# A planner of instruction order is given a margin behind the landing of loads and a limit on side products

## The chip, the cores and the metric

The kernel runs on one core of a Trainium2 chip. The metric is the device time of one execution in microseconds (us), given as the median of several runs; a profile of one further execution is read beside it.

## What is computed

Two layers of a hybrid decoder trunk, for a prompt of 256 tokens and for 8 sample tokens (one step each), all in float32. Each layer is

```python
h = rms_norm(x, norm_w)
z = einsum('btd,dc->btc', h, w_in)                 # 2048 -> 7296 columns, split among the branches
y_a = rwkv_time_mix(z_a, ...)                      # 12 heads x 64: token shift, delta-rule matrix state, group norm
y_b = attention_branch(z_b, ...)                   # 12 heads x 64: dilated windows (prompt), cache of past rows (sample)
y_c = pool_branch(z_c, ...)                        # causal multi-scale mean pooling
mix = concatenate([y_a, y_b, y_c])                 # each branch multiplied by SiLU of its own gate columns
y = x + einsum('btc,cd->btd', mix, w_out)          # 2048 -> 2048
```

and the new states (matrix state, shifted row, pooling rows, new keys and values) are outputs too.

## The kernel before

Work is held with channels on the 128 partitions and the 264 tokens (256 + 8) in the free dimension. The two big projections are the **stream** (`stream`, line 301): weights come in pieces of 512 KB (`raw`, four blocks of 128 rows by 256 columns, three buffers), ScalarE rounds a piece to float32r (`hi`), VectorE makes the rest (`lo <- raw - hi`), and TensorE adds hi x xh, hi x xl and lo x xh into a PSUM tile of tag `acc` (three buffers, two of them in use for a pair of column tiles). A stream matmul is 128x128 by 128x264. In the output projection the moving operands are the mix tiles `mh`/`ml` (branch A), `mb` (branch B) and `mc` (branch C), and `stream` takes the quarters in the order 2, 1, 3, 0, so that the later half of `mb` is read first.

All other TensorE work is **side products**, into PSUM tiles of tag `a` (five buffers): transposes, the low-rank products, the delta-rule chunks, the attention scores and values. The parts of a layer follow each other in the program like this:
- `up_load` loads the raw up matrices (`rwkv_w_up`, `rwkv_a_up`), which are cast to `up`; the scale of the rows (`x_done`, `row_scale`, tiles `ss`, `rtok`, `dg`, `rstd`) is made in the same stretch, and every projected tile `z` is multiplied by `rstd`.
- `a_k`, `a_kdone`, `a_r`, `a_solve` build the chunk matrices. They go through DRAM (`g_dram`) and come back as `xm`, which a loop of 15 steps on VectorE inverts in blocks of 16 (tile `tm`); the results go through DRAM again and come back as `ra`, `rat`, `rb`, `rbt` (in the tile `iv`), `x16` and `x32`.
- `invert` (line 525) makes the inverses of 64 x 64 from these by four products, each of 12 x 4 small matmuls: `x16` with `rat`, `y16` with `right`, `x32` with `rbt`, `y32` with `rb`. Then `a_chain` runs the chunks.
- `b_prompt` is the attention of the prompt and `b_sample` that of the sample tokens. `b_sample` takes six pairs of `kc` (cache, by GpSimd's queue) and `qb` (queries spread over the partitions, by SyncE's queue) and then three groups of two `vc`; all these tiles have the tag `c4` with three buffers.
- `a_mix`, `b_mix`, `c_gate` write the mix tiles; then comes the output projection.

The order of the instructions on each engine is not that of the program. After the program is built, the class `Plan` (line 1336) takes all instructions, their dependences, the buffer rings and a cost for each, and simulates the engines (`once`, line 1554): at each point of plan time every free engine takes the ready instruction with the longest tail of work behind it. `apply` then fixes each engine's order by this plan. On the chip an engine runs its queue strictly in that order and waits where an operand is late.

TensorE has two ready lists in the plan, stream and side. A side product is begun when a run of them is on, when one has been ready for `wait` = 1500 ns, or when `batch` = 400 ns of them are ready; else a stream matmul is taken, and if there is none, a side product after all. A `bundle` is a row of side matmuls that is kept together (`self.after`, `forced`). A load is taken to land at a modelled time (`fin`), and its consumers become ready `slack` later: 0 for what the stream itself needs (`feeds`: the operands of stream matmuls' own predecessors such as the casts), `care` = 1200 ns on TensorE and `margin` = 200 ns elsewhere. The plan is made twice: after the first pass no load that isn't a weight piece may be issued earlier than 12 us before its first consumer (`ahead`).

Of the kernel before, what the change touches and what calls it, by code (L numbers as in the profile page):

```python
# [3 lines left out]

# [1331 lines left out]
class Plan:  # L1336
# [200 lines left out]
                tail[q] = max(tail[q], t)  # L1537
        return tail

    def run(self, factor=1, hop=300, margin=200, batch=0, wait=0, switch=0, quiet=0, lead=1, dyn=(), ahead=0, care=350):  # L1540

        self.hold = [0.0] * self.n
        args = factor, hop, margin, batch, wait, switch, quiet, lead, dyn, care
        if ahead:
            self.once(*args)
            for k, i in enumerate(self.ins):
                if self.dma[k] and not self.feeds(k):
                    self.hold[k] = max(0.0, min([self.start[q] for q in self.after_load[k]], default=0.0) - ahead)
        return self.once(*args)
# [1 line left out]
    def feeds(self, k):  # L1551
        return self.tag[self.first_out[k]].startswith("raw") if self.first_out[k] in self.tag else False

    def once(self, factor, hop, margin, batch, wait, switch, quiet, lead, dyn, care):
        n, eng, preds, dma, dur, stream = self.n, self.eng, self.preds, self.dma, self.dur, self.stream
        spare = {t: d for t, r in self.ring.items() for m, d in dyn if t.split("_" + self.pool[r[0]])[0] == m}
        tail = self.tails(factor, hop, spare)
# [2 lines left out]
        feeds = {q for k in range(n) if stream[k] for q in preds[k]}  # L1560
        slack = [0 if stream[k] or k in feeds else care if eng[k] == "PE" else margin for k in range(n)]
# [32 lines left out]
        hw = bus_free = now = 0.0  # L1594
        start, fin, order = [0.0] * n, [0.0] * n, {e: [] for e in free}
        taken = {"DVE": 0.0, "POOL": 0.0}
        release = []
        last_use = defaultdict(float)
        done, since, side_on, last_stream, forced = 0, None, False, False, None
        claims = {k: [t for t in ts if t in left] for k, ts in self.claim.items()}  # L1600
# [15 lines left out]
        def take(h):  # L1616
            while h:
                p, k = heapq.heappop(h)
                w = blocked(k)
                if w is None:  # L1620
                    return k
                parked[w].append(k)
            return None

        def unpark(key):
            for k in parked.pop(key, ()):
                heapq.heappush(ready[queue(k)], (prio[k], k))

        while done < n:
            while pending and pending[0][0] <= now + 1e-9:  # L1630
                _, k = heapq.heappop(pending)
                heapq.heappush(ready[queue(k)], (prio[k], k))
            while release and release[0][0] <= now + 1e-9:
                _, t = heapq.heappop(release)
                free_slots[self.tag[t]] += 1
                open_tiles[self.pool[t]] -= 1
                unpark(self.tag[t])
                unpark("pool " + self.pool[t])
            moved = False
            for e in free:  # L1640
                if free[e] > now + 1e-9 or (e == "SP" and hw > now + 700):
                    continue
                if e == "PE" and forced is not None:
                    k = forced
                elif e == "PE":
                    h = ready["SIDE"]
                    if h and since is None:
                        since = now
                    k = None
                    if h:  # L1650
                        go = side_on or h[0][0] < -2e9 or now - since >= wait or sum(dur[x[1]] for x in h) >= batch
                        if go:
                            k = take(h)
                            if k is not None:
                                side_on = True
                                since = None
                    if k is None:
                        k = take(ready["PE"])
                        if k is None and h:
                            k = take(h)  # L1660
                        if k is not None and stream[k]:
                            side_on = False
                            since = since if h else None
                else:
                    k = take(ready[e])
                if k is None:
                    continue
                for t in claims.get(k) or touches[k]:
                    if t not in live:
                        live.add(t)  # L1670
                        tag = self.tag[t]
                        while next_tile[tag] < len(self.ring[tag]) and self.ring[tag][next_tile[tag]] in live:
                            next_tile[tag] += 1
                        free_slots[tag] -= 1
                        unpark(tag)
                start[k] = now
                if dma[k]:
                    if e == "SP":
                        hw = max(hw, now) + 470
                        free[e] = now + 60  # L1680
                        begin = max(hw + 650, bus_free)
                    else:
                        free[e] = now + 520
                        begin = max(now + 1690, bus_free)
                    bus_free = begin + bust[k]
                    fin[k] = bus_free + 908
                else:
                    extra = 0
                    if e == "PE" and stream[k] != last_stream:
                        extra = switch if stream[k] else 0 if k in claims else switch / 2  # L1690
                    elif self.port[k]:
                        extra = max(0.0, taken["POOL" if e == "DVE" else "DVE"] - now)
                    free[e] = fin[k] = now + dur[k] + extra
                    if self.port[k]:
                        taken[e] = fin[k]
                if e == "PE":
                    last_stream = stream[k]
                    forced = self.after.get(k)
                order[e].append(k)
                done += 1  # L1700
                moved = True
                out = list(succ[k])
                if stream[k]:
                    nstream += 1
                    out += held.pop(nstream, ())
                for q in out:
                    r = fin[k] if dma[k] else fin[k] + (100 if eng[q] == "SP" else HOP[e, eng[q]])
                    if e != eng[q] or dma[k]:
                        r += slack[q]
                    est[q] = max(est[q], r)  # L1710
                    count[q] -= 1
                    if not count[q] and q != forced:
                        heapq.heappush(pending, (est[q], q))
                for t in touches[k]:
                    left[t] -= 1
                    last_use[t] = max(last_use[t], fin[k] + (0 if dma[k] else 150 if e == "PE" else 100))
                    if not left[t]:
                        heapq.heappush(release, (last_use[t], t))
            if moved:
                continue  # L1720
            c = [x for x in free.values() if x > now + 1e-9]
            if pending:
                c.append(pending[0][0])
            if release:
                c.append(release[0][0])
            if hw > now + 700:
                c.append(hw - 700)
            c = [x for x in c if x > now + 1e-9]
            if not c:
                raise RuntimeError(f"no order found: {done} of {n} {dict((a, len(b)) for a, b in parked.items())}")  # L1730
            now = min(c)
# [68 lines left out]
def build(nc, shapes, depth=DEPTH):  # L1800
    ins = {n: nc.dram_tensor(f"in_{n}", s, F32, kind="ExternalInput").ap() for n, s in shapes.items()}
    outs = {n: nc.dram_tensor(f"out_{n}", s, F32, kind="ExternalOutput").ap() for n, s in _OUTS}
    with tile.TileContext(nc, schedule_with_timeline_sim=True) as tc, ExitStack() as ctx:
        trunk = Trunk(ctx, tc, ins, outs, depth)
        trunk.run()
        plan = Plan(tc, trunk.bundles)
        plan.run(ahead=12000, care=1200, batch=400, wait=1500, switch=105, margin=200, hop=180, factor=0.9, lead=25, quiet=60, dyn=[("a", 2)])
        plan.apply()


# [10 lines left out]
```

## Time and profile before

| | us |
|---|---|
| median of 3 runs | 1086.47 |
| lowest and highest run | 1085.95, 1093.89 |
| the profiled execution's own time | 1087.3 |
| its span, first to last instruction | 1085.5 |
| TensorE busy in it (share) | 1045.3 (96%) |
| VectorE, ScalarE busy | 856.8 (79%), 546.3 (50%) |
| mean granted TensorE clock | 0.992 |

The span is the time between the first and the last instruction; the execution's own time also holds what lies around it. Layer 0 lasts to about 552 us of the span, layer 1 from there to the end.

### The profile page before, as it was taken

To read this page: it belongs to the slowest core of one execution; us is meant where nothing else is said; L and a number is where in the kernel's file an instruction comes from. 1 tells how busy PE (TensorE), PEld (TensorE's weight loads), DVE (VectorE), ACT (ScalarE), POOL (GpSimd) and SP (SyncE) were. 2 spreads that over 40 slices of the span, in tenths; PEclk is the share of its full clock that TensorE was granted. 3 is DMA by queue.
4 is the path that set the end of the run, shared out by engine and by line. 5 is a ranking of instruction groups with operands and counts; after the bars stand their busy time and mean duration, and the time that the engine had idled before them with its cause. 6 is when DMAs were issued, how large, how long until landed. Compare 5 with 4: busy or idle time off the path is not lost.

```text
span 1085.5 us, 24558 instructions
## 1 busy us (share of the span) xinstructions
PE 1045.3 (96%) x9802; PEld 997.2 (92%) x9802; DVE 856.8 (79%) x1684; ACT 546.3 (50%) x934; POOL 136.3 (13%) x262
## 2 busy tenths in 40 slices
PE   9999999889998999999999999989999999989998
PEld 8899898889897987999999998989898998979998
DVE  7769977989997898766666799689997999886443
ACT  7546434354655474444545464334537465734332
POOL 0003210100012101000110042112000231010000
PEclk9999999999999999999999999999999999999999
DMA  7654489797467865577775545797984488655774
GB/s 273 203 156 144 148 250 247 212 237 233 135 190 244 267 186 179 178 231 224 228 238 160 174 133 174 229 263 214 254 239 137 149 255 297 204 177 173 232 226 149
DMA packets 154683, 223.64 MB, mean 206 GB/s; under 512 B 75984, under 2 KB 109152, under 8 KB 154552
## 3 DMA queue, kind: packets, MB, share of 16 engines
q1 hardware_dynamic: 146456, 195.94, 60.5%
q0 software_dynamic: 8112, 26.12, 7.2%
q8 instruction: 77, 1.26, 0.5%
q14 instruction: 38, 0.31, 0.1%
HBM read 198.55 MB, written 24.03 MB: 205 GB/s over the span
## 4 chain that ended last, share of the span: by engine, by line
PE 53%; DVE 23%; DMA 12%; issue 5%; ACT 5%; SPq 1%; DVEq 0%; ACTq 0%; POOLq 0%
PE acc L323 46%; DVE lo L140 7%; PE a L115 6%; DMA raw<-in_w_in 3%; DMA qb<-q_dram 2%; ACT hi L137 2%; PE a L118 2%; DVE z L140 2%; SPq L155 1%; DVE tm L140 1%; DMA svec<-sk_dram 1%; DVE s L140 1%; DMA rwkv_a_up<-in_rwkv_a_up 1%; DMA res<-resid 1%; DMA q_dram<-brows 1%
## 5 line engine op out<-in xcount | busy, mean ns | idle before, releaser
L323 PE MATMUL acc<-xh,hi 128*128 128x264 f32 x1824 | 473.2, 289 | 6.6 <-DVE z L140 3.3
L323 PE MATMUL acc<-xl,hi 128*128 128x264 f32 x1824 | 473.2, 290 | 0.0
L137 ACT ACTIVATE hi<-raw 128x1024 fp32r<-128x1024 f32 (+1 forms) x296 | 309.8, 1046 | 323.1 <-PE acc L323 228.2
L140 DVE TENSOR_TENSOR lo<-raw,hi 128x1024 fp32r<-128x1024 f32 (+1 forms) x296 | 356.9, 1206 | 137.2 <-ACT hi L137 136.2
L323 PEld LDWEIGHTS acc<-xh,hi 128*128 128x128 f32 x1824 | 346.0, 190 | 12.8 <-ACT hi L137 4.4
L323 PEld LDWEIGHTS acc<-xl,hi 128*128 128x128 f32 x1824 | 346.2, 190 | 5.0 <-issue 3.7
L323 PE MATMUL acc<-xh,lo 128*128 128x264 f32 x1824 | 295.6, 289 | 2.3 <-DVE lo L140 2.1
L323 PEld LDWEIGHTS acc<-xh,lo 128*128 128x128 f32 x1824 | 249.9, 190 | 8.1 <-DVE lo L140 3.9
L323 PE MATMUL acc<-mb,hi 128*128 128x264 f32 x384 | 57.3, 284 | 0.3 <-DVE xs L140 0.2
L140 DVE TENSOR_TENSOR z<-acc,rstd 128x264 f32<-128x264 f32 (+1 forms) x112 | 51.7, 466 | 5.2 <-ACT rstd L137 2.1
L323 PEld LDWEIGHTS acc<-mb,hi 128*128 128x128 f32 x384 | 50.9, 188 | 0.8 <-DVE xs L140 0.8
L323 PE MATMUL acc<-mh,hi 128*128 128x264 f32 x192 | 49.5, 284 | 0.0
L323 PE MATMUL acc<-ml,hi 128*128 128x264 f32 x192 | 49.4, 285 | 0.0
L353 POOL COPY zcol<-z 128x9 f32<-128x9 f32 x50 | 20.2, 404 | 219.1 <-DVE z L140 209.6
L323 PEld LDWEIGHTS acc<-ml,hi 128*128 128x128 f32 x192 | 36.2, 188 | 0.0
L323 PEld LDWEIGHTS acc<-mh,hi 128*128 128x128 f32 x192 | 36.1, 188 | 0.0
L323 PE MATMUL acc<-mb,lo 128*128 128x264 f32 x192 | 33.8, 285 | 0.0
L323 PE MATMUL acc<-mh,lo 128*128 128x264 f32 x192 | 33.6, 283 | 0.0
L323 PE MATMUL acc<-mc,hi 128*128 128x264 f32 x256 | 33.5, 283 | 0.0
L323 PEld LDWEIGHTS acc<-mc,hi 128*128 128x128 f32 x256 | 32.0, 188 | 0.0
L140 DVE TENSOR_TENSOR xs<-acc,res 128x264 f32<-128x264 f32 x32 | 13.5, 433 | 22.1 <-DMA res<-resid 16.0
L323 PEld LDWEIGHTS acc<-mh,lo 128*128 128x128 f32 x192 | 27.6, 188 | 0.0
(357 smaller groups left out, 1309.1 us busy)
## 6 DMA issues: line engine op xcount, KB each, us to landing
raw<-in_w_in SPq DMA_DIRECT2D x224, 512.0 KB, 3.6
raw<-in_w_out SPq DMA_DIRECT2D x64, 512.0 KB, 3.6
g_dram<-gs SPq DMA_DIRECT2D x8, 768.0 KB, 6.9
gs<-g_dram SPq DMA_DIRECT2D x8, 768.0 KB
kc<-in_cache_k_w POOLq DMA_DIRECT2D x12, 512.0 KB, 5.6
qb<-q_dram SPq DMA_DIRECT2D x12, 512.0 KB, 4.5
vc<-in_cache_v_w POOLq DMA_DIRECT2D x12, 512.0 KB, 4.5
s<-in_state_wkv POOLq DMA_DIRECT2D x12, 256.0 KB, 4.3
```

The source lines that it names most:

```text
L115: self.note(self.nc.tensor.matmul(out, lhsT, rhs, start=start, stop=stop))
L118: self.note(self.nc.tensor.transpose(out, in_, self.c("ident")[base:base + k, base:base + k]))
L137: self.nc.scalar.activation(out, in_, func, **kw)
L140: self.nc.vector.tensor_tensor(out, a, b, op=op)
L155: self.nc.sync.dma_start(out, in_)
L323: self.nc.tensor.matmul(accs[t][:, :T], a[:, k4, cs], b[k], start=first, stop=q == order[3] and k4 == 3 and late == 1)
L353: self.nc.gpsimd.tensor_copy(self.zcol[:, :, a], z[:, NP - 1:T])
```

## The change

Two parameters are added to the planner, and the call sets `far=1500` and `dense=100`. With `far`, a consumer of a load becomes ready 1500 ns later in the plan than before, unless it is one that the stream needs directly (`feeds`) or stands on SyncE or GpSimd. With `dense`, the planner keeps the begin times of all side matmuls of the last 8000 ns of plan time (`recent`), and does not take a side product ahead of the stream while there are 100 or more; the path that takes one because no stream matmul is ready, and the later members of a bundle, are as before. No instruction is added or removed.

```diff
@@ run, once: two more parameters
-    def run(self, factor=1, hop=300, margin=200, batch=0, wait=0, switch=0, quiet=0, lead=1, dyn=(), ahead=0, care=350):
+    def run(self, factor=1, hop=300, margin=200, batch=0, wait=0, switch=0, quiet=0, lead=1, dyn=(), ahead=0, care=350, far=0, dense=10 ** 9):
...
-        release = []
+        release, recent = [], deque()
...
                     k = None
-                    if h:
+                    while recent and recent[0] < now - 8000:
+                        recent.popleft()
+                    if h and len(recent) < dense:
                         go = side_on or h[0][0] < -2e9 or now - since >= wait or sum(dur[x[1]] for x in h) >= batch
...
                 if e == "PE":
                     last_stream = stream[k]
+                    if not stream[k]:
+                        recent.append(now)
                     forced = self.after.get(k)
...
                     if e != eng[q] or dma[k]:
-                        r += slack[q]
+                        r += slack[q] + (far if dma[k] and q not in feeds and eng[q] != "SP" and eng[q] != "POOL" else 0)
...
-        plan.run(ahead=12000, care=1200, batch=400, wait=1500, switch=105, margin=200, hop=180, factor=0.9, lead=25, quiet=60, dyn=[("a", 2)])
+        plan.run(ahead=12000, care=1200, far=1500, dense=100, batch=400, wait=1500, switch=105, margin=200, hop=180, factor=0.9, lead=25, quiet=60, dyn=[("a", 2)])
```

## Rows read from the trace of the kernel before

**Rows 1.** The page, part 1: busy us (share of the span) of TensorE and VectorE

```profile
PE   1045.3 (96%) x9802; PEld 997.2 (92%) x9802; DVE 856.8 (79%) x1684; ACT 546.3 (50%) x934; POOL 136.3 (13%) x262
```

**Rows 2.** TensorE in windows: length, busy us (matmuls), granted clock, DMA share, GB/s

```profile
40.00:48.00 8.00, 6.37 (x39) 0.79 0.33 91
...
216.00:224.00 8.00, 7.80 (x224) 0.79 1.14 249
...
760.00:768.00 8.00, 5.82 (x205) 0.96 1.09 267
768.00:776.00 8.00, 8.00 (x138) 0.83 0.89 251
...
968.00:976.00 8.00, 5.64 (x48) 0.97 0.78 261
976.00:984.00 8.00, 8.00 (x57) 0.82 0.45 132
```

**Rows 3.** TensorE's timeline: start, length, instruction, [idle time before it <- releaser]

```profile
42.37 0.39 PE L323 MATMUL acc<-xh,hi 128*128 128x264 f32 x1 [1.63 <-DVE z L140]
...
216.20 1.31 PE L115 MATMUL a<-rat,x 32*32 32x16 f32 x96 [3.68 <-DMA rat<-rat_dram]
...
226.22 1.02 PE L115 MATMUL a<-iv,x 32*32 32x32 f32 x96
...
229.37 0.37 PE L115 MATMUL a<-iv,y 32*32 32x32 f32 x18
...
232.29 0.87 PE L115 MATMUL a<-iv,y 32*32 32x32 f32 x78 [2.55 <-issue]
...
428.93 0.64 PE L115 MATMUL a<-vc,ppad 128*32 128x256 f32 x8 [1.32 <-DMA vc<-in_cache_v_w]
...
569.00 0.39 PE L323 MATMUL acc<-xh,hi 128*128 128x264 f32 x1 [0.95 <-DVE z L140]
...
755.20 0.99 PE L115 MATMUL a<-rat,x 32*32 32x16 f32 x96
...
765.47 1.17 PE L115 MATMUL a<-iv,x 32*32 32x32 f32 x96 [2.18 <-DVE s L140]
...
963.46 0.64 PE L115 MATMUL a<-vc,ppad 128*32 128x256 f32 x8 [0.40 <-DMA vc<-in_cache_v_w]
...
974.20 0.64 PE L115 MATMUL a<-vc,ppad 128*32 128x256 f32 x8 [1.72 <-DMA vc<-in_cache_v_w]
```

**Rows 4.** Who waited for whom: us in total, times, longest us

```profile
ACT ra L137 <- DMA ra<-ra_dram: 7.8, 2, 4.7
...
DVE kc L140 <- DMA qb<-q_dram: 5.8, 6, 1.8
...
ACT up L137 <- DMA rwkv_w_up<-in_rwkv_w_up: 4.0, 2, 2.2
DVE tm L140 <- DMA xm<-g_dram: 4.0, 2, 2.1
```

**Rows 5.** Instructions with mb, 400 to 470 us: durations ns, first and last start

```profile
L323 PE MATMUL acc<-mb,hi x32: 281/284/288, 457.5 to 469.9; 128*128 128x264 f32 x32
...
L140 DVE TENSOR_TENSOR mb<-sgb,mb x6: 419/427/434, 422.3 to 439.4; 128x264 fp32r<-128x264 f32 x6
```

**Rows 6.** The same for 960 to 1010 us (layer 1)

```profile
L323 PE MATMUL acc<-mb,hi x48: 281/284/323, 988.1 to 1004.5; 128*128 128x264 f32 x48
...
L140 DVE TENSOR_TENSOR mb<-sgb,mb x6: 425/426/434, 967.0 to 984.9; 128x264 fp32r<-128x264 f32 x6
```

**Rows 7.** DMA issues: count, KB each, median us from issue to landing

```profile
x<-x_dram SPq DMA_DIRECT2D x2, 192.0 KB, 5.1
```

**Rows 8.** SyncE's timeline at 760 us: start, length, instruction

```profile
760.25 0.43 SPq L155 DMA_DIRECT2D x<-x_dram  x1
```

**Rows 9.** ScalarE's timeline at 764 us

```profile
764.76 1.06 ACT L137 ACTIVATE hi<-raw 128x1024 fp32r<-128x1024 f32 x1 [3.61 <-DMA raw<-in_w_in]
```

More of the change, by code (lines that the diff above doesn't have):

```diff
@@ L1 @@
 import heapq
-from collections import Counter, defaultdict
+from collections import Counter, defaultdict, deque
 from contextlib import ExitStack, contextmanager
@@ L1538, in tails @@
         return tail
-    def run(self, factor=1, hop=300, margin=200, batch=0, wait=0, switch=0, quiet=0, lead=1, dyn=(), ahead=0, care=350):
+    def run(self, factor=1, hop=300, margin=200, batch=0, wait=0, switch=0, quiet=0, lead=1, dyn=(), ahead=0, care=350, far=0, dense=10 ** 9):
         self.hold = [0.0] * self.n
-        args = factor, hop, margin, batch, wait, switch, quiet, lead, dyn, care
+        args = factor, hop, margin, batch, wait, switch, quiet, lead, dyn, care, far, dense
         if ahead:
@@ L1552, in feeds, with once @@
         return self.tag[self.first_out[k]].startswith("raw") if self.first_out[k] in self.tag else False
-    def once(self, factor, hop, margin, batch, wait, switch, quiet, lead, dyn, care):
+    def once(self, factor, hop, margin, batch, wait, switch, quiet, lead, dyn, care, far, dense):
         n, eng, preds, dma, dur, stream = self.n, self.eng, self.preds, self.dma, self.dur, self.stream
```

## The prediction

> **What bounds the kernel now.** Four kinds of view, in this order. First the busy shares of the page: TensorE is busy 1045.3 us of the 1085.5 us span and VectorE 856.8 us [rows 1]. TensorE's work does not change (the edit touches only the order), so what can be won is the 40.2 us in which TensorE is idle, plus what its clock costs, and the rest is fixed. Second, TensorE alone in windows of 8 us [rows 2]: the granted clock is 0.79 in the window at 40 us, 0.79 at 216, 0.96 and 0.83 at 760 and 768, and 0.97 and 0.82 at 968 and 976. [...] Each costs (1 - 0.79) x 8 = 1.7 us of full-speed time (0.04 + 0.17 and 0.03 + 0.18 of a window make the same). Third, TensorE's instructions in order of time with the idle time before them [rows 3]: before each of those falls stands a gap, 1.63, 3.68, 2.18 and 1.72 us long. A gap that goes or gets much shorter therefore gives back its own length and perhaps 1.7 us more. Fourth, who waits for loads [rows 4]: ScalarE waits 7.8 us for ra and 4.0 us for the first raw up matrix, over both layers, VectorE 5.8 us for qb and 4.0 us for xm. An engine runs its queue in order, so such a wait also holds the hi and lo casts behind it, and without casts TensorE's stream stops.
>
> The second thing to see is what the end of each layer hangs on. The last write of mb (the attention part of the mix) starts at 439.4 us in layer 0 and 984.9 us in layer 1 and takes 0.43 us; the first output matmul that reads mb starts at 457.5 and 988.1 us [rows 5, 6]. So the side chain ends 17.7 us early in layer 0 and only 2.8 us early in layer 1.
>
> **The margin behind landings (far).** It adds 1.5 us to the time at which the planner thinks a loaded tile can be used, for consumers on TensorE, ScalarE and VectorE that do not feed the stream directly. It adds no instruction and no wait. It moves these consumers back in their queue, behind other work that the plan has ready at that time; loads on SP and GpSimd are not given the margin themselves, though they follow the new order. The x32 load shows how late data really comes: 192 KB takes 5.1 us from issue to landing [rows 7]. A consumer that now stands at the head of a queue for longer than 1.5 us gets at most 1.5 us of that back, one that waits less gets all of it. By place, first layer 0:
> - up matrices: they stand in front of the chain that makes the row scale, and the first scaled z releases TensorE after 1.63 us at 42.37 [rows 3]. ScalarE waits 4.0 / 2 = 2.0 us there in a layer [rows 4], more than that, so the gap can go whole, and its clock fall with it: 1.63 + 1.7 = 3.3 us.
> - rat and ra: TensorE waits 3.68 us at 216.20 [rows 3], and ScalarE holds a hi cast behind ra. 1.5 us comes back; 2.2 us of gap stays, so I leave the clock fall in: 1.5 us (the other end is 3.68 + 1.7 = 5.4).
> - vc: 1.32 us at 428.93 [rows 3], all of it: 1.3 us.
> - xm: VectorE waits 2.0 us in each layer [rows 4], of which 1.5 us comes back to VectorE; it is busy 79% of the span [rows 1], so between nothing and 1.5 us reaches TensorE and I take the middle, 0.75 us.
>
> Layer 1: 0.95 us before the scaled z at 569.00, vc 0.40 us at 963.46 and 1.5 of the 1.72 us at 974.20 with its clock fall of 1.7 us [rows 2, 3], and 0.75 us for xm: 5.3 us. The gap of 2.18 us at 765.47 I count at nothing. It is put down to VectorE, but the product reads x32, whose load is issued at 760.25 and takes about 5.1 us [rows 7, 8], so it is a landing. Yet at the same time the next hi cast waits 3.61 us for its own raw tile and ends only at 765.8 [rows 9]: TensorE would have had nothing else to run. Its other end is 2.18 + 1.7 = 3.9 us.
>
> **The limit on side products (dense).** At most 100 side matmuls may begin in 8 us of plan time while a stream matmul is ready; the later members of a bundle are exempt, and so is TensorE with no stream work. The densest stretch is the block inverse, four products of 12 x 4 = 48 matmuls (a row counts 96: each fp32 matmul of the program is two in the trace). Two products fit under the limit, so the third may begin 8 us after the first at the earliest. On the chip it stands 226.22 - 216.20 = 10.0 us behind it in layer 0 and 765.47 - 755.20 = 10.3 in layer 1 [rows 3]; at that spacing the limit hardly binds. In the plan, which knows no late landing, the products may stand closer. So it costs the chain between nothing and 8 less two products of 1.31 us, 5.4 us; I take nothing, by the rows. What it may give: the fourth product stops for 2.55 us at 232.29, after 18 of its 96 equal matmuls, and the profile shows nothing that it waits for ("issue") [rows 3]. I read this as instructions that had not arrived, because the first 18 and the other 78 read the same two tiles. Spread out, they should not outrun their delivery: between 0 and 2.55 us, in layer 0 alone. As the limit binds so little I take half, 1.3 us. [...]
>
> **What both cost.** They make the side chain longer in the plan. In the sample attention six pairs of kc and qb go through three buffers one after the other: 6 x 1.5 = 9.0 us for each layer, of which 5.8 / 2 = 2.9 us is waited already [rows 4]; 6.1 is left. Three groups of vc make 3 x 1.5 = 4.5, less the 1.3 us waited in layer 0 and 2.1 in layer 1: 3.2 and 2.4. In layer 0 that is 9.3 us, with the limit's bound 14.7, against 17.7 us of early end [rows 5]: other stream work stands in front of the output matmuls, and the cost is nothing. In layer 1 it is 8.5 us against 2.8 [rows 6]: between 0 (the chain's own hops get shorter where queues wait less) and 5.7 us. No row decides between these ends, so I take the middle, 2.9 us.
>
> Sum: layer 0 gives 3.3 + 1.5 + 1.3 + 0.75 + 1.3 = 8.2 us, layer 1 gives 5.3 - 2.9 = 2.4: 10.6 us less. The profiled execution took 1087.3 us (1.8 us outside its span), 0.8 us above the median of 1086.47, so 1087.3 - 10.6 - 0.8 = 1076 us.
>
> **Rivals.** (1) The chain of layer 1 is not the bound, because work on it also loses its waits: both layers give their gains in full, 8.2 + 5.3 = 13.5, so 1073 us; with the rest of the gaps at 216.20, 232.29 and 765.47 and their clock falls (2.2 + 1.7 + 1.3 + 3.9 = 9.1) 1064. For it: the twelve qb loads are waited for 0.5 us each [rows 4], so they hardly pace the chain. Against it: the 2.8 us of [rows 6].
> (2) Slower: the kc/qb ring, vc and the limit stretch layer 1's side chain by all they can, 9.0 + 4.5 + 5.4 = 18.9 us, TensorE runs out of stream work before mb is ready and stands still for 18.9 - 2.8 = 16.1 us. With layer 0's gains that is 1087.3 + 16.1 - 8.2 - 0.8 = 1094 us, without them 1103. It turns to a loss as soon as the chain grows by more than 2.8 + 8.2 = 11.0 us. For it: the small margin, and that the planner adds the same 1.5 us where the wait is short. Against it: layer 0 does the same steps with 17.7 us to spare.
> (3) Nothing: a load lands no sooner, and where no cast is ready, as at 765.47 [rows 9], a consumer moved back leaves the same hole under another name: 1086 us, give or take 3. Against it: at 216.20 a hi cast stood behind ra.
> (4) The change doesn't do what it says: if the plan has the consumers of late loads more than 1.5 us behind their landing already, order and waits stay. It gives 1086 too and goes with (3).
>
> **How the numbers follow.** Forecast, 1073 to 1081: 0.37. Rival 1, 1063 to 1073: 0.22. Rivals 3 and 4, 1082 to 1089: 0.20. Rival 2, 1087 to 1103: 0.21, half of it above 1097. A measurement of this kernel tells about 1%, 10.9 us, from no change: below 1075.6 lie rival 1 and some two fifths of the forecast's case, 0.22 + 0.16 = 0.38; above 1097.3 lies 0.10; the rest, 0.52, is between. The range takes in rival 1's end and rival 2 up to 1097: 1063 to 1097, with about one in ten left out.
>
> **What would show it.** Right: TensorE's idle time falls from 40 to some 33 us, the gap before the first z at 42 us is gone and the one inside a product too; ScalarE's wait for ra is shorter by 3 us over both layers; the mean clock rises from 0.992 by two falls fewer. Wrong: ra, vc and up are waited for as long as before; or a new gap of many us stands before the first output matmul of layer 1, with mb ready only after the stream in front of it has ended. The forecast fails above all if the new order, which changes everywhere after the first moved consumer, makes casts late in places where they are in time now.

## The result and the profile after

The changed kernel takes 1075.58 us (median of 5 runs, 1069.25 to 1076.72) against 1088.83 (median of 5, 1085.95 to 1093.89): ratio 0.9862, 95% interval 0.9828 to 0.9897, so 1.0 to 1.7% faster. Ratios compare fast executions only; of those reported here two of nudge's twelve, which its median includes, were slow. The profiled execution took 1076.72 us, its span 1074.8 at a mean clock of 0.995.

The first part of the page of after, engines' busy time:

```profile
PE 1041.3 (97%) x9802; PEld 995.4 (93%) x9802; DVE 857.8 (80%) x1684; ACT 547.8 (51%) x934; POOL 143.7 (13%) x262
```

Against [rows 1] TensorE has the same 9802 matmuls. Its span is 10.7 us shorter, in two parts: its idle time fell from 40.2 to 33.5 us (6.7), and its busy time by 4.0 us. The same matmuls in less time points to the clock (mean 0.995 after, 0.992 before): TensorE in windows of 8 us (length, busy us and matmuls, granted clock, DMA share, GB/s), all windows within the span of after that hold a fall:

```profile
224.00:232.00 8.00, 7.59 (x216) 0.79 1.02 284
...
344.00:352.00 8.00, 6.57 (x52) 0.97 0.95 328
352.00:360.00 8.00, 8.00 (x57) 0.82 0.87 280
...
744.00:752.00 8.00, 7.08 (x163) 0.79 1.13 229
```

The falls of [rows 2] at 40 and at 968 to 984 are gone; those at 216 and 760 are now at 224 and 744; the one at 344 was there before too, though neither [rows 2] nor the prediction has it. In the trace of before:

```profile
344.00:352.00 8.00, 4.20 (x32) 0.93 0.87 288
352.00:360.00 8.00, 8.00 (x62) 0.86 0.74 232
```

So five falls became three. In the traces' records of the granted clock each of these eight is 3.41 us at 0.50, and (1 - 0.50) x 3.41 = 1.7 us; two falls at 1.7 us are 3.4 of the 4.0 us.

TensorE's timeline of after at the places of [rows 3] (start, length, instruction, idle time before it and its releaser):

```profile
39.00 0.39 PE L323 MATMUL acc<-xh,hi 128*128 128x264 f32 x1 [1.09 <-ACT hi L137]
...
41.70 0.39 PE L323 MATMUL acc<-xh,hi 128*128 128x264 f32 x1 [0.46 <-DVE z L140]
...
214.32 1.31 PE L115 MATMUL a<-rat,x 32*32 32x16 f32 x96 [0.84 <-DMA rat<-rat_dram]
...
223.81 1.11 PE L115 MATMUL a<-iv,x 32*32 32x32 f32 x96 [1.77 <-DVE nwt L140]
...
230.07 0.61 PE L115 MATMUL a<-iv,y 32*32 32x32 f32 x47 [0.41 <-issue]
...
560.10 0.39 PE L323 MATMUL acc<-xh,hi 128*128 128x264 f32 x1 [0.95 <-DVE z L140]
...
745.69 1.31 PE L115 MATMUL a<-rat,x 32*32 32x16 f32 x96 [0.92 <-DMA rat<-rat_dram]
...
752.63 0.65 PE L115 MATMUL a<-right,y 32*32 32x16 f32 x56 [0.40 <-issue]
...
758.89 0.57 PE L115 MATMUL a<-iv,x 32*32 32x32 f32 x43 [2.64 <-issue]
...
765.28 0.25 PE L115 MATMUL a<-iv,y 32*32 32x32 f32 x5 [1.92 <-issue]
```

No vc stands there any more. The inverse of layer 0 lost 6.23 us to gaps before (3.68 + 2.55) and loses 3.02 now (0.84 + 1.77 + 0.41). That of layer 1 had 2.18 at 765.47 and now has 0.92 + 0.40 + 2.64 + 1.92 = 5.88: worse by 3.7 us, and three of its four gaps are of the kind "issue", inside a product.

Who waited for whom in after:

```profile
PE a L115 <- issue: 5.4, 4, 2.6
...
DVE kc L140 <- DMA qb<-q_dram: 1.7, 2, 1.2
...
ACT ra L137 <- DMA ra<-ra_dram: 1.5, 2, 0.9
...
ACT up L137 <- DMA rwkv_w_up<-in_rwkv_w_up: 1.4, 1, 1.4
```

The waits of [rows 4] fell, ra from 7.8 to 1.5 us, qb from 5.8 to 1.7, up from 4.0 to 1.4; xm (4.0) is no longer listed.

The instructions with mb, at the end of each layer's side chain (ns, first and last start), layer 0 and then layer 1:

```profile
L323 PE MATMUL acc<-mb,hi x48: 281/283/288, 449.4 to 465.8; 128*128 128x264 f32 x48
...
L140 DVE TENSOR_TENSOR mb<-sgb,mb x6: 424/426/434, 428.5 to 445.4; 128x264 fp32r<-128x264 f32 x6
...
L323 PE MATMUL acc<-mb,hi x72: 281/283/288, 978.2 to 1006.2; 128*128 128x264 f32 x72
...
L140 DVE TENSOR_TENSOR mb<-sgb,mb x6: 423/426/434, 956.3 to 974.2; 128x264 fp32r<-128x264 f32 x6
```

The first output matmul of layer 0 comes 8.1 us earlier than in [rows 5], that of layer 1 9.9 us earlier than in [rows 6]. The first z of layer 1 comes 8.9 us earlier (569.00 before, 560.10 after), and the span ends 10.7 earlier. So layer 0 with its output projection gave 8.9 us and layer 1 gave 1.8. In layer 0 the chain ends 6.0 us later than before (445.4 for 439.4) and is 3.6 us early instead of 17.7; in layer 1 it ends 10.7 us earlier, 8.9 of which is the layer's earlier start, and is 3.6 us early instead of 2.8.

### The profile page after: what moved, and what is told of

Its sections match the earlier page's. It is cut to its first block, busy times and chain, and to the rows that moved or that the text cites. A ratio compares the mean times of both kernels' runs of the same rounds, so it can differ in the third digit from the quotient of the medians.

```text
span 1074.8 us, 24548 instructions
## 1 busy us (share of the span) xinstructions
PE 1041.3 (97%) x9802; PEld 995.4 (93%) x9802; DVE 857.8 (80%) x1684; ACT 547.8 (51%) x934; POOL 143.7 (13%) x262
## 3 DMA queue, kind: packets, MB, share of 16 engines
q8 instruction: 77, 1.26, 0.5%
## 4 chain that ended last, share of the span: by engine, by line
PE 64%; DVE 18%; DMA 9%; ACT 4%; issue 4%; SPq 1%; POOL 0%; DVEq 0%; ACTq 0%; POOLq 0%
PE acc L323 55%; PE a L115 7%; DMA raw<-in_w_in 6%; DVE lo L140 5%; PE a L118 2%; ACT hi L137 2%; DVE s L140 1%; DVE z L140 1%; DMA iv<-rb_dram 1%; SPq L155 1%; DVE bk L149 1%; DMA pool<-in_pool_w 1%; DVE tm L140 1%; DVE bk L140 1%; ACT uv L137 1%
## 5 line engine op out<-in xcount | busy, mean ns | idle before, releaser
L323 PE MATMUL acc<-mc,hi 128*128 128x264 f32 x256 | 33.5, 283 | 0.0
L140 DVE TENSOR_TENSOR s<-s,svec 128x512 f32<-128x512 f32 x36 | 24.4, 683 | 4.8 <-DMA s<-in_state_wkv 1.7
```

What stands on the lines that cost most here:

```text
L140: self.nc.vector.tensor_tensor(out, a, b, op=op)
L323: self.nc.tensor.matmul(accs[t][:, :T], a[:, k4, cs], b[k], start=first, stop=q == order[3] and k4 == 3 and late == 1)
```

## The experiments

The theory: consumers of late loads stood too far ahead in their queues, and the margin takes them out of the way; the limit adds little. Its rivals: the limit made the gain; or any new order of this plan would have given it. Edits are against the changed kernel unless said otherwise; "no dense" drops the limit. Each ratio is against the kernel before on the same chip.

### The two parts alone

**far_only**, no dense:

```diff
-        plan.run(ahead=12000, care=1200, far=1500, dense=100, batch=400, ...
+        plan.run(ahead=12000, care=1200, far=1500, batch=400, ...
```

> The margin of 1500 ns without the limit on side products. If the margin makes the gain (my theory), the ratio to the kernel before is 0.984 to 0.990, as with both (0.986). If the limit makes it, 0.997 to 1.003. TensorE's order is that of the changed kernel up to the fourth product of the inverse in layer 0 (some 228 us), so up to there the gaps must be those of the changed kernel: 0.8 us before the first product, none of 2 us or more before 223 us. Without the limit I expect gaps inside the four products of 2 to 3 us, as before, in sum no larger than with both (5.4 us).

**dense_only**, the limit without the margin:

```diff
-        plan.run(ahead=12000, care=1200, far=1500, dense=100, batch=400, ...
+        plan.run(ahead=12000, care=1200, dense=100, batch=400, ...
```

> The limit of 100 side products in 8 us without the margin. If the margin makes the gain, the ratio is 0.995 to 1.005 and ScalarE waits for ra for 7 to 8 us and TensorE 3.7 us for rat, as before. If the limit makes the gain, the ratio is 0.984 to 0.990 and the gap of 2.55 us in the fourth product of layer 0 is gone. If gains come from any rearrangement of the order, it may fall anywhere between 0.985 and 1.015 while the waits for ra and rat stay.

**dense50**, `dense=50` beside the margin:

> Margin 1500 and a limit of 50 instead of 100 (100 small matmuls as the trace counts them). If the gaps in the middle of products are instructions that arrive late, and spreading cures it, the five gaps put down to issue (0.41, 0.40, 2.64, 1.92, and 1.77 at the start of the third product) shrink from 7.1 us to under 3, and the ratio to before is 0.979 to 0.986. If they are something else, or if the chain of products becomes longer by what the gaps lose, the ratio stays at 0.984 to 0.992.

Measured: far_only 1071.45 us, 0.9841 (0.9815 to 0.9868); dense_only 1083.59 us, 0.9947 (0.9927 to 0.9968); dense50 1079.51 us, 0.9911 (0.9881 to 0.9941). The margin alone gives all of the gain. The limit alone gives 0.5% and keeps the late loads: ra is waited for 5.4 us, rat for 3.41, and the 1.63 us before the first z stay. Beside the margin it gives nothing that can be measured, and at 50 the time is longer than with the margin alone.

Two things here vary without the edit. On TensorE far_only has the order of after up to 228 us, and yet the first product waits 0.84 us for rat in after and not at all in far_only, where the same 0.8 us was expected. And dense_only has the order of before up to 233 us, and yet its fourth product of layer 0 does not stop. So a single gap of this size in one profile is not proof of what an edit does.

The gaps of the kind "issue" in far_only's timeline:

```profile
228.56 1.33 PE L115 MATMUL a<-iv,y 32*32 32x32 f32 x81 [3.55 <-issue]
...
749.39 0.68 PE L115 MATMUL a<-right,y 32*32 32x16 f32 x60 [1.33 <-issue]
...
755.00 0.60 PE L115 MATMUL a<-iv,x 32*32 32x32 f32 x46 [0.45 <-issue]
...
760.57 0.65 PE L115 MATMUL a<-iv,y 32*32 32x32 f32 x32 [2.09 <-issue]
```

They are 7.4 us where no more than the 5.4 of after were expected, so the limit may take something from them: 2.0 us, with no gain in the time. In dense50 none is left, but its side chain is late: its timeline has these two gaps, each before a matmul that reads mb, which neither far_only nor a kernel with the limit at 100 has:

```profile
448.25 1.41 PE L323 MATMUL acc<-mb,hi 128*128 128x264 f32 x6 [1.86 <-ACT mb L137]
...
975.82 1.40 PE L323 MATMUL acc<-mb,hi 128*128 128x264 f32 x6 [2.04 <-ACT mb L137]
```

They are 3.9 us. The profiled execution of dense50, 1073.92 us, is the fastest of its six, so where the rest of the 8 us between its median and that of far_only lies is not shown.

### What the "issue" gaps are

**shift40** puts 40 small matmuls at the start, at no cost in the plan; apart from them the order on each engine is that of after.

```diff
+            for _ in range(40):
+                self.mm(pu[:, :8], calmr[:, :P], calmr[:, :8])
...
+        for k, i in enumerate(self.ins):
+            if type(i).__name__ == "InstMatmult" and width(list(i.outs)[0]) == 8 and k < self.first:
+                self.dur[k] = 0.0
```

> The changed kernel with 40 matmuls of 8 columns more at the start of TensorE, planned at no cost, so that every engine's order is otherwise the same. In the changed kernel gaps without a releaser stand after 2008, 6714, 6841 and 6968 matmuls of the trace: distances of 127. If they are blocks of instructions that arrive late, they stand after the same counts here, that is 40 matmuls earlier in the work: in layer 1 some 13 matmuls into the third product instead of 53. If they belong to the products or their data, they stay after the 53rd. The time is that of the changed kernel within 1% on either theory (40 more matmuls cost at most 3 us at the start).

One execution took 1083.46 us. That is 0.7% more than after, lost at the start, where 3 us were expected and the small matmuls cost some 8 us (the first scaled z releases TensorE at 49.73 instead of 41.70), so its time says nothing of the gaps. Their places do. In its timeline:

```profile
230.18 0.37 PE L115 MATMUL a<-right,y 32*32 32x16 f32 x21 [2.41 <-issue]
...
237.13 0.33 PE L115 MATMUL a<-iv,x 32*32 32x32 f32 x7 [3.31 <-issue]
```

They stand at other instructions than those of after. What is the same is the count. Windows from the start of the span to just before a gap count the matmuls (x...) ahead of it. Before, up to the gap at 232.29:

```profile
0.00:232.28 232.28, 219.29 (x2008) 0.99 0.70 208
```

After, up to those at 223.81, 230.07, 752.63, 758.89 and 765.28:

```profile
0.00:223.80 223.80, 213.68 (x1880) 1.00 0.69 206
0.00:230.06 230.06, 219.53 (x2008) 0.99 0.70 208
0.00:752.62 752.62, 732.73 (x6714) 0.99 0.69 207
0.00:758.88 758.88, 736.35 (x6841) 0.99 0.69 208
0.00:765.27 765.27, 740.83 (x6968) 0.99 0.70 209
```

shift40, up to 230.18, 237.13 and 771.64:

```profile
0.00:230.17 230.17, 220.15 (x1881) 0.98 0.65 197
0.00:237.12 237.12, 223.80 (x2009) 0.98 0.66 200
0.00:771.63 771.63, 747.81 (x6968) 0.99 0.68 205
```

far_only has 2008, 6715, 6843 and 6970. The stops at about 2008 and 6968 kept their counts in shift40, 40 matmuls earlier in the work; the one at 1881 is new, 128 before the one at 2009. Those at 6714 and 6841 did not come back: the expectation's place, 13 matmuls into the third product of layer 1, has no stop. So not every such count stops, but the stops stand on counts 127 or 128 apart, whatever the instruction. The pages of before and after list 77 packets and 1.26 MB for the instruction queue, and 9802 / 127 = 77.2.

The trace has the packets themselves, and they settle it. In after such packets landed at 228.60, 751.09, 757.22 and 763.77 us, and the four stops ended at 230.07, 752.63, 758.89 and 765.28. In the fourteen traces together, all 44 gaps over 0.2 us that the views put down to "issue" ended 1.1 to 1.7 us after a packet of the instruction queue had landed. From stop to stop in after (752.62 to 758.88 and on to 765.27) the windows count 127 matmuls and 127 weight loads. So the reading is that TensorE's instructions come in packets of 127 matmuls with their weight loads, and at these 44 gaps it stood because one was used up before the next was there. In after three packets in a row were begun 6.3 and 6.4 us apart (752.63, 758.89, 765.28), in far_only 5.6 us. A dense product uses 96 of the 127 in 1.0 to 1.3 us.

The gap of 1.77 at 223.81 lies on such a count too, but it is another thing: the last packet had landed 3.1 us before its end. The third product reads x32, issued at 215.17, and the last update of that load's semaphore came at 223.68, 0.13 us before the product began. far_only shows the same at the same product; its load, issued at 213.01, has its landing in the view of DMA issues, and 213.01 + 8.3 = 221.3:

```profile
x<-x_dram SPq DMA_DIRECT2D x2, 192.0 KB, 8.3
...
221.47 1.11 PE L115 MATMUL a<-iv,x 32*32 32x32 f32 x96 [1.59 <-DVE nwt L149]
```

So in layer 0 one load is late in spite of the margin, and the VectorE that the view names is not what ended the wait.

### Is it any new order? And how much margin?

**nudge** is the kernel before with the margin on the other engines moved by 60 ns, which changes TensorE's order throughout:

```diff
-        plan.run(ahead=12000, care=1200, batch=400, wait=1500, switch=105, margin=200, ...
+        plan.run(ahead=12000, care=1200, batch=400, wait=1500, switch=105, margin=260, ...
```

> A control: the kernel before with the planner's small margin of 200 ns raised to 260 ns, for consumers of other engines' results and of loads alike. Far too little to cover a late landing, but it reorders as many instructions as the change does. If any rearrangement may give or take 1 to 2%, the ratio to the kernel before falls outside 0.993 to 1.007. If the margin of 1500 ns works by covering late landings, the ratio here is 0.993 to 1.007, with waits for ra, rat, vc and up as before (ra 5 to 8 us, rat 2 to 4 us).

**far750**, **far1200**, **far2000** and **far3000** set `far` to 750, 1200, 2000 and 3000, no dense.

> Half the margin (750 ns), no limit on side products. If the gain comes from covering late landings, about half of the gain of 1.6% with 1500 ns: ratio 0.988 to 0.994, wait for ra between 1.7 and 7.8 us, some 4 us. If it is a matter of order alone, no relation to the size: as likely above 0.995 as below 0.985.

> Margin 1200 ns alone. If the gain is a plateau that is reached once the late landings are covered, a ratio of 0.983 to 0.990 here and with 2000 ns. If 1500 ns hit a lucky order, the neighbours have nothing to do with it: about 0.995 to 1.003, as with 750 ns (0.9987).

> Margin 2000 ns alone. If the side chain grows with the margin until it is the bound (3000 ns: 1.003, with gaps of 7 to 9 us in front of each output projection), the last write of mb ends in layer 1 later against the first output matmul than with 1500 ns (3.6 us before it), but a gap of no more than 3 us appears: ratio 0.985 to 0.993. On the lucky-order theory anything from 0.985 to 1.003, with no relation to the end of the chain.

> Twice the margin (3000 ns), no limit on side products. The waits for ra, rat, up and vc are gone (under 1 us each), but the side chain is longer in the plan by up to another 13 us for each layer. If the chain then ends behind the stream work in front of the output projection, a gap of 3 us or more stands before the first output matmuls and the ratio is 0.987 to 1.000, worse than the 0.984 of 1500 ns. If the chain is not the bound, 0.978 to 0.984.

Measured, with the waits from each one's profile (vc: TensorE's wait), and by how much mb is ready ahead of the first output matmul of layer 1 (last write plus 0.43 us; below zero it is read in part before all of it is there):

| `far`, ns | us | ratio (95%) | ra | vc | issue | mb ahead |
|---|---|---|---|---|---|---|
| 0 (nudge) | 1091.50 | 1.0001 (0.9973 to 1.0029) | 4.4 | 2.8 | 4.4 | 6.0 |
| 750 | 1087.54 | 0.9987 (0.9966 to 1.0007) | 4.2 | 3.7 | 8.5 | 3.6 |
| 1200 | 1076.27 | 0.9880 (0.9862 to 0.9898) | 1.3 | 0.6 | 6.8 | 2.4 |
| 1500 (far_only) | 1071.45 | 0.9841 (0.9815 to 0.9868) | 1.7 | 0.5 | 7.4 | 3.6 |
| 2000 | 1075.33 | 0.9867 (0.9846 to 0.9888) | none | none | 6.8 | -6.3 |
| 3000 | 1093.44 | 1.0030 (1.0009 to 1.0051) | none | 0.8 | 2.5 | -8.8 |

This new order alone, the only one tried without a purpose, gives nothing. Its waits for ra and rat were expected to stay and are 3.4 and 2.4 us shorter, but in a profiled execution of 1083.38 us, well below its median, so they say little of its usual time. far750 was expected to give half of the gain and gives none. Its profiled execution, 1088.26 us, is near its median: ra's wait is 3.6 us shorter than before, rat's 3.1 and that for the first up matrix 2.6, and yet TensorE is idle for 42.1 us (40.2 before), 8.5 of it at stops for instructions (2.6 before). The gain is there from 1200 ns, where ra and vc are nearly covered, and holds to 2000. It does not need every wait to go: in far1200 ScalarE waits 5.3 us for the first raw up matrix, more than the 4.0 before. At 3000 the late loads are gone and the time is above that of before, and above the 1.000 that was expected at most. The timeline of far3000 shows where it goes:

```profile
447.95 2.19 PE L323 MATMUL acc<-mb,hi 128*128 128x264 f32 x8 [3.27 <-ACT mb L137]
...
454.82 0.59 PE L118 MATMUL a<-cbase,os 128*128 128x128 f32 x2 [2.26 <-ACT os L137]
...
984.02 0.69 PE L118 MATMUL a<-cbase,os 128*128 128x128 f32 x2 [4.53 <-ACT os L137]
...
992.08 0.69 PE L118 MATMUL a<-cbase,os 128*128 128x128 f32 x2 [2.26 <-ACT os L137]
```

TensorE has no stream work left and waits for the last steps of the sample attention. With two gaps of 0.78 and 1.10 us more in layer 0 and two of 1.09 and 1.10 in layer 1 it is 7.4 and 9.0 us. Its clock falls with them, in windows of 8 us:

```profile
448.00:456.00 8.00, 4.38 (x26) 0.72 0.31 102
456.00:464.00 8.00, 7.49 (x42) 0.64 0.10 23
...
984.00:992.00 8.00, 4.71 (x26) 0.50 0.34 115
992.00:1000.00 8.00, 6.82 (x38) 0.64 0.00 0
```

What the lower clock costs is read from the busy time: 1046.0 us in far3000 (mean clock 0.984) and 1039.5 in far_only (0.992), 6.5 us more. Idle time is 45.3 and 30.1 us, 15.2 more, and the gaps above are 16.4. Together 21.7 us: far3000 is 1.9% (some 21 us) above far_only by their ratios. far2000 has the first signs of the same in layer 1 (2.21 us before os at 972.80, 1.57 before mb at 975.05).

### Which consumers need it

Three kernels, no dense, with 1500 ns for some consumers only: **far_noc4** for all but those of kc, qb and vc, **far_c4** for those alone, **far_nope** for all but TensorE's.

```diff
-                        r += slack[q] + (far if dma[k] and q not in feeds and eng[q] != "SP" and eng[q] != "POOL" else 0)
+                        r += slack[q] + (far if dma[k] and q not in feeds and eng[q] != "SP" and eng[q] != "POOL" and not (self.tag.get(self.first_out[k]) or "").startswith("c4") else 0)
```

far_c4 has the same term without `not`, far_nope has `and eng[q] != "PE"` in its place.

> Margin 1500 ns, no limit, but not for the cache and query tiles of the sample attention (kc, qb, vc). The order is that of the margin alone up to about 345 us. If the margin on these tiles costs the chain of layer 1 some 6 to 8 us, the last write of mb in layer 1 comes earlier by 3 us or more after the start of the layer than with the margin everywhere, and vc is waited for on TensorE again (2 to 4 us in sum): the ratio stays within 0.004 of 0.984. If the gain sat in these tiles, it rises to 0.990 or more; if it sat in the front parts (up, ra, rat, xm), it is 0.980 to 0.988.

> Margin 1500 ns only for kc, qb and vc of the sample attention, no limit; the complement of the run that leaves them out (0.9911). If the two shares add up to the 1.6% of the margin everywhere, 0.991 to 0.995, with vc no longer waited for on TensorE and the waits for ra, rat, up as before (7.8, 3.7, 4.0 us). If the share of these tiles came from order alone, 0.997 to 1.003.

> Margin 1500 ns for consumers on ScalarE and VectorE but not on TensorE, whose consumers had 1200 ns already; no limit. If the casts that stood behind ra and the up matrices matter most, 0.984 to 0.988 though TensorE waits for rat and vc again (3 to 6 us together). If TensorE's own waits matter as much as I put them in the sum (1.5 us at rat, 4.5 at vc with a fall of the clock), 0.988 to 0.993.

Measured: far_noc4 1079.99 us, 0.9911 (0.9887 to 0.9935); far_c4 1081.72 us, 0.9946 (0.9925 to 0.9967); far_nope 1075.62 us, 0.9880 (0.9850 to 0.9910). The first two are 0.9 and 0.5%, together the 1.6% of far_only within their intervals: neither group alone makes the gain. But 0.5% is also what the limit gives with the late loads in place, so a part of that size may be order alone. ScalarE's and VectorE's consumers seem to carry most of it (1.2 of 1.6%, with intervals that overlap), though in far_nope TensorE still waits 3.1 us for vc and ScalarE 3.9 for ra. Two things speak against reading causes off places. far_nope has these waits nearly as long as far750 (3.7 and 4.2 us) and gains where far750 does not. And in far_noc4 the margin spares vc, where 2 to 4 us of waiting were expected, and TensorE's wait for vc is 0.3 us all the same: a wait that is gone need not have gone by the margin on its own load. The profiled execution of far_c4 took 1090.39 us, 0.8% above its median, so no row of it is used.

## Why the prediction was right, and which of its terms were not

The forecast was 1076 us, and 1075.58 was measured; the idle time was to fall to some 33 us and fell to 33.5, with two falls of the clock fewer. The kind of gain was right, but that the numbers meet so closely is in part luck. The forecast starts from a median of 1086.47 us; against the 1088.83 of the result the gain is 13.3 us and not 10.4, and 1076 / 1086.47 = 0.990 lies just outside the interval of the ratio. Between the profiled executions it is 10.6 us, as in the sum, but not from the sum's places: those listed below gave some 6.6 us of the span's 10.7 (xm left out), and some 4 came elsewhere. The largest piece of these stands in front of the prompt's attention in layer 0, where gaps of 1.06 us at 345.36 and 2.74 at 350.77 became one of 1.43 at 350.66. In layer 1 two terms failed most, the limit and the price on the chain, and they nearly cancel.

- **What bounds the kernel**: right. The gain is idle time of TensorE (6.7 us) and busy time (4.0 us), of which two falls of the clock are 3.4. Rival 3 (a consumer moved back leaves the same hole) is refuted by the margins of 1200 to 2000 ns; 750 ns came out as it says.
- **up and the first z**: 3.3 us predicted, 2.0 found. The 1.63 us and a gap of 0.21 us at 35.94 became 1.09 + 0.46, so only 0.3 of idle time went, and the fall of the clock (1.7).
- **rat and ra**: 1.5 us predicted, 2.8 found (3.68 to 0.84), and the fall of the clock behind this gap went with it. Another fall stands 8 us later, behind the new gap of 1.77 us for x32, so that 1.8 us is lost again. "A consumer that now stands at the head of a queue for longer than 1.5 us gets at most 1.5 us of that back" was too low a bound: ScalarE's wait for ra fell by 6.3 us over two layers. nudge's profile lacks 3.4 us of it by a new order alone, so the split between the two is open.
- **vc**: 1.3 us in layer 0, and 0.4 + 1.5 + 1.7 in layer 1, predicted; 1.3 and 0.40 + 1.72 + 1.7 found. By far_noc4 this need not be vc's own margin.
- **The first z of layer 1**: 0.95 us predicted, nothing found. The gap is 0.95 us at 560.10, as it was at 569.00.
- **xm**: its wait went. 0.75 us a layer was an allowance. TensorE's gaps in the stretch behind it went from 1.9 to 2.6 us in layer 0 (177 to 183 us of before) and from 2.9 to 1.2 in layer 1 (707 to 722); that xm is the cause is not shown.
- **The limit**: the step that failed. Half of the stop of 2.55 us at 232.29 was to come back, in layer 0 alone. 0.41 is left there, though dense_only shows that this stop can also be missing in the old order. But in layer 1, which had no such stop, the products have three, 4.96 us. They do not come from the limit, as far_only has 3.87 us there (1.33 + 0.45 + 2.09), and they do not need the margin either, as nudge has 2.50 (0.78 + 1.21 + 0.51): products that wait less for data run into the delivery of instructions. That this is why layer 1 had none before is argued, not shown. The reading of the stop was right ("instructions that had not arrived"); that 100 matmuls in 8 us would keep within the delivery was not. 100 of the program are 200 in the trace, and a packet holds 127, as the counts show: at the 6.3 us between packets in after some 160 arrive in 8 us (an estimate, 127 / 6.3 x 8). 50 are 100, and dense50 has no stop. A packet is 1.26 MB / 77 = 16.4 KB, and its delivery shows in the time here, by gaps of 0.2 to 3.6 us on these counts.
- **The price on the chain**: in layer 0 it was to grow by up to 14.7 us at no cost; it ends 6.0 us later and costs nothing. In layer 1 the 2.9 us (the middle of 0 and 5.7) did not come: there the chain ends 1.8 us earlier against the layer's start, and the row that the argument hung on, 2.8 us of margin, became 3.6. That was rival 1's reason, and it held for the chain; rival 1's time did not come, since the inverse took back 3.7 us in that layer and the first z gave nothing.
- **Rival 2** (the side chain outlasts the stream) did not happen at 1500 ns, but its mechanism is real: far3000 is it, 0.3% slower than before, with 9.0 us of gaps in layer 1 where 16.1 were feared for the worst case. Layer 0, with 17.7 us to spare, fell to it too.

Open: why the limit alone gives 0.5% with the late loads still in place, how far order without a purpose can move the time (one nudge is one sample), and how the gain splits between single loads, since each edit changes the order everywhere behind it. That the margin makes the gain is shown; through which waits it does so is not. The best version found is the margin without the limit, 0.9841; its interval overlaps that of the change.

## What to carry to other kernels

Where a planner fixes the order of in-order queues, give its model the landing times that the trace shows: a consumer at the head of a queue too early blocks work that is ready. In before ScalarE stood idle for 4.74 us for ra until 216.58, and the next hi cast began behind it, at 218.03, though its raw piece had landed by 213.5 us. Try the size of the margin: here 1200 to 2000 ns paid 1.2 to 1.6%, 750 nothing, 3000 a loss, and neither the longest waits before (3.7 us for rat, 4.7 for ra) nor the time by which the side chain ended ahead of the stream (17.7 and 2.8 us) would have given it. Test such an edit against a nudge that changes the order alone, and go by the time: waits can shrink and the time stay, as with 750 ns.

## What the runs showed that was not expected

- In these runs TensorE stopped 44 times for 0.2 to 3.6 us and went on 1.1 to 1.7 us after a packet of instructions had landed; the view calls it "issue". Stops next to each other stood 127 or 128 matmuls apart in after, far_only and shift40. The dense small products reached this, with 127 matmuls in 5.6 to 6.4 us; with a limit of 50 in 8 us of the plan (dense50) there was none.
- A wait that a view puts down to VectorE can be a landing: at 223.81 in after the load of x32 landed 8.5 us after its issue (5.1 in [rows 7]), and the view names nwt.
- In after the length of a gap does not tell whether the clock falls. 0.92 us at 745.69 stands beside a fall (0.50 for 3.41 us from 747.43), and at 2.64 us at 758.89 there is none (1.00 in the windows at 752 and 760).
- In shift40 the granted clock falls to 0.50 with TensorE busy: after the 40 small matmuls at the start and with no idle time in the records (a record's end is modelled), TensorE in windows of 8 us; the loss is (0.13 + 0.50 + 0.01) x 8 = 5.1 of the 8 us that the 40 cost:

```profile
8.00:16.00 8.00, 8.00 (x58) 0.87 0.96 347
16.00:24.00 8.00, 8.00 (x37) 0.50 0.16 59
24.00:32.00 8.00, 8.00 (x67) 0.99 0.59 198
```
